# Hybrid attention layer on one core: biases and evictions' stores over ScalarE's queue, later pairs' values in four blocks, decay ranks stored split

## The chip, the core and the metric

The kernel runs on one core of a Trainium2 chip. The core has a matrix engine (TensorE, PE in the profile, with PEld for its weight loads), a vector engine (VectorE, DVE), an activation engine (ScalarE, ACT), a general one (GpSimd, POOL) and one that only issues transfers (SyncE, SP). Each engine works through its own instructions in order and waits on semaphores for the others. DMAs between HBM and the on-chip memory are instructions too: they stand in the queue of the engine that issues them, and the 16 DMA engines of the core do the moving. The metric is the device time of one execution in microseconds.

## The reference, cut to what matters

One encoder layer on 1024 tokens (a grid of 16 rows and 64 columns) of width 1024, in float32: a half-step FFN, a mixer, a half-step FFN, each followed by a scaled residual and a layer norm. The mixer adds two branches, neighbourhood attention (8 heads, a window of 8 x 16 tokens, a bias for each relative offset) and gated linear attention (GLA, 4 heads, two directions), each gated by its own sigmoid:

```python
def reference(x, ...):
    x = layer_norm(ALPHA * x + 0.5 * swiglu_ffn(x, ...), ln1_g, ln1_b)
    x = layer_norm(ALPHA * x + hybrid_mixer(x, w_in, ...), ln2_g, ln2_b)
    x = layer_norm(ALPHA * x + 0.5 * swiglu_ffn(x, ...), ln3_g, ln3_b)

def hybrid_mixer(h, w_in, na_rpb, ...):
    proj = h @ w_in
    na_q, na_k, na_v, g_q, g_k, g_v, g_g, dlf, dlb, gate_na, gate_gla = split(proj)
    y_na = neighborhood_attention(na_q, na_k, na_v, na_rpb) @ w_branch_na
    y_gla = gla_bidirectional(g_q, g_k, g_v, g_g, dlf, dlb, ...) @ w_branch_gla
    merged = sigmoid(gate_na) * y_na + sigmoid(gate_gla) * y_gla
    return merged @ w_out

# neighbourhood attention, per query: scores over its 8 x 16 keys
scores = einsum('bhqd,bhiqjd->bhqij', q_r, k_sel) + bias
p = softmax(scores); out = einsum('bhqij,bhiqjd->bhqd', p, v_sel)
# GLA: decay gates of low rank, per direction
log_a = log_sigmoid(dec_lr @ w_dec2 + b_dec) / 16
```

## The kernel before

Every float32 matmul is done as three: an operand is split into a rounded part and the rest (`split`, L130: ScalarE copies, VectorE subtracts), and high x high, high x low and low x high are added in PSUM. A unit of such work over 512 columns is a "step" of three matmuls; the kernel counts time in such steps (`STEP` = 0.65 units each).

**What sets the order.** TensorE's instructions stand in program order. The code for the dense matmuls are generators that yield after each step; `run` (L189) advances a clock by the step's cost and, when it has passed the time of an entry in a list (`at`, L184), lets that entry write its instructions there. So attention and GLA are threaded between dense matmuls by a table of numbers: `NA_T0` and `NA_DT` for the attention, `GLA_*` for GLA. The instructions of the other engines, DMAs among them, are placed by a scheduler.

**The mixer's stages.** After the first FFN, `tok_major` (L855) computes the attention's values by token and stores them to `vscr`; `decay_rank` (L956) computes the 32 decay ranks and stores them to `dls`; `pairs` (L882) computes queries, keys and the rest. Then comes the attention stage (L1127 to L1134). Its dense work, through which the attention is threaded, is `tok_major` for GLA's values (stored to `gv`, 8 tiles) and four `gate_gla` (stored to `gts`). Each tile of 128 x 512 is evicted by ScalarE into a buffer `sl` (two of them, `stage`, L425) and stored from there by a DMA on SyncE's queue (L877, L1125).

**The attention.** There are 64 items: four pairs of heads, for each two halves of the grid's rows, four blocks of columns, two heads. Item i goes through a chain of engines: `na_scores` (L1047: two matmuls on TensorE, the bias added and the minimum taken on VectorE, the exponential on ScalarE, the normalisation on VectorE), two items later `na_transpose` (L1076: three transposes on TensorE into `pt`, copied out by ScalarE), and an item after that `na_values` (L1087). One item begins every `NA_DT` units. The bias of an item comes from HBM (`bias_tile`, L1039, into `bt`, two buffers), 288 or 384 KB for two or four items; it is asked for when the bias before it comes into use:

```python
if hh == 0 and b != 2:
    na_b[0] = na_b.pop("next")
    if i < 62:
        bias_tile(i + (2 if b != 1 else 4))
```

**The pairs.** `qk_pair` (L1000) loads a pair's queries, keys and values: 13 DMAs for `q`, `k` and `kl` on GpSimd's queue (L1006), and 16 for the values `vp` on SyncE's queue (L1027 to L1031), each of 96 or 128 rows of 512 bytes. For pairs 1 to 3 this happens 10.5 items before the pair's first; GpSimd writes a mark into each tile first (L1010 to L1014), which holds the DMAs back until the item reached by then has its softmax.

**GLA's start.** After the attention, the decay ranks come back from `dls` and are split into a tile `dlT` (L1161 to L1168: two DMAs, four copies on ScalarE, two subtractions on VectorE). `gla_decay` (L1175) of the first head multiplies them (`zs`, L1188) at `GLA_D0`, and at `GLA_T0` the head's first transposes (`kps`, L1224) need the outcome of that chain; the next heads follow every `GLA_DT`.

Of the kernel before, what the change touches and what calls it, by code (L numbers as in the profile page):

```python
# [8 lines left out]
F32 = mybir.dt.float32  # L9
F32R = mybir.dt.float32r  # L10
BF16 = mybir.dt.bfloat16
U32 = mybir.dt.uint32
AF = mybir.ActivationFunctionType
ALU = mybir.AluOpType
# [4 lines left out]
P = 128  # L19
D = 1024  # L20
S = 1024
KD = D // P
HF = 512
# [12 lines left out]
NEG = -1.0e30  # L36
HOIST = 100
WARM = 30
GLA_D0 = 8.5
GLA_T0 = 29.5  # L40
GLA_DT = 30.3
GLA_NEXT = 8.5
GLA_OUT = (15.0, 28.3, 28.3, 35.5)
NA_T0 = 20.0
NA_DT = 0.94
NA_GATES = (4, 5, 6, 7)
GLA_GATES = (1, 2, 3)
FIRST = (1, 2, 4, 8)
# [12 lines left out]
COL0 = (0, 8, 24, 40)  # L61
COLW = (24, 32, 32, 24)
BOFF = (0, 288, 288, 672)
# [4 lines left out]
def hybrid_layer(ctx, tc, xT, wg1, wu1, wds1, wd1, wg2, wu2, wds2, wd2, wcol, wnv, wgv, wdl, wgate,  # L68
                 wbr, wout, lnp, bias, dec2, bdec, ng, ident_d, masks_d, ln3, outN):
    nc = tc.nc  # L70
# [4 lines left out]
    def pool(stack, name, bufs=1, space=None):  # L75
        kw = dict(name=name, bufs=bufs)
        if space is not None:
            kw["space"] = space
        if space is not DRAM:
            kw["reuse_waits"] = "tile"  # L80
        return stack.enter_context(tc.tile_pool(**kw))
# [9 lines left out]
    dram = pool(ctx, "dram", 1, DRAM)  # L91
# [3 lines left out]
    def nm(s):  # L95
        uid[0] += 1
        return f"{s}_{uid[0]}"
# [32 lines left out]
    def split(src, hi, lo):  # L130
        nc.scalar.activation(hi, src, AF.Copy)  # L131
        nc.vector.tensor_tensor(lo, src, hi.bitcast(F32), ALU.subtract)  # L132
# [29 lines left out]
    for c1 in FIRST:  # L162
        w = slice(c0 * P, c1 * P)
# [20 lines left out]
    def at(delay, fn):  # L184
        uid[0] += 1
        pending.append((clock[0] + delay, uid[0], fn))
        pending.sort(key=lambda e: e[:2])
# [634 lines left out]
    one = Ffn(ffn1, x, xr, half(xT), wg1, wu1, wds1, wd1, 0)  # L822
# [19 lines left out]
    ogs = dram.tile([4, P, S], F32, tag="ogs", name="ogs")  # L842
    gts = dram.tile([KD, P, S], F32, tag="gts", name="gts")

    dls = dram.tile([32, S], F32, tag="dls", name="dls")


    def tok_weights(w_d, n):
# [6 lines left out]
    def tok_major(w_d, dst, alloc=None, wq=None):  # L855
        wq = wq or tok_weights(w_d, 4 if alloc is None else 2)
        for i in range(len(wq) // 2, 4):
            raw = wpool.tile([P, D], F32, tag="raw", name=nm("raw"), bufs=2)
            with tc.high_priority(offset=HOIST):
                nc.sync.dma_start(raw, w_d[i])  # L860
                for o in (0, HF):
                    wq.append(alloc())
                    split(raw[:, o:o + HF], *wq[-1])
        for t in range(8):
            h, c = t // 4, (t % 4) * P
            ps = dps()
            for k in range(KD):
                xh, xl = x1[k][h]
                wh, wl = wq[k]
                a, b = xh[:, c:c + P], xl[:, c:c + P]  # L870
                nc.tensor.matmul(ps, a, wh, start=k == 0, stop=False)
                nc.tensor.matmul(ps, a, wl, start=False, stop=False)
                nc.tensor.matmul(ps, b, wh, start=False, stop=k == KD - 1)
                yield STEP
            sb = stage()
            nc.scalar.activation(sb, ps, AF.Copy)
            nc.sync.dma_start(dst(t), sb)  # L877

    unblk = lambda t: t.rearrange("p (b r c) -> p r b c", r=8, b=4)

# [75 lines left out]
    def decay_rank():  # L956
        raw = wpool.tile([P, KD, 32], F32, tag="raw", name=nm("raw"), bufs=2)
        nc.sync.dma_start(raw, wdl)
        w = wpool.tile([P, KD, 64], F32R, tag="wh", name=nm("wh"))
        nc.scalar.activation(w[:, :, 0:32], raw, AF.Copy)  # L960
        nc.vector.tensor_tensor(w[:, :, 32:64], raw, w[:, :, 0:32].bitcast(F32), ALU.subtract)
        for h in range(2):
            ps = dps((64, HF))
            for k in range(KD):
                xh, xl = x1[k][h]
                if k:
                    nc.tensor.matmul(ps[0:32], w[:, k - 1, 0:32], x1[k - 1][h][1], start=False,
                                     stop=False)
                if k == KD - 1:
                    nc.tensor.matmul(ps[0:32], w[:, k, 0:32], xl, start=False, stop=False)  # L970
                nc.tensor.matmul(ps, w[:, k], xh, start=k == 0, stop=k == KD - 1)
                yield STEP * 2 / 3
            sb = stage()
            nc.scalar.activation(sb[0:32], ps[32:64], AF.Copy)
            nc.vector.tensor_tensor(sb[0:32], sb[0:32], ps[0:32], ALU.add)
            nc.sync.dma_start(dls[:, h * HF:(h + 1) * HF], sb[0:32])

    run(tok_major(wnv, lambda t: vscr[t * P:(t + 1) * P, :], one.hpair))
    assert not pending
# [13 lines left out]
    vgrid = vscr.rearrange("(r c) e -> r c e", c=64)  # L993
    nap = ExitStack()
    npool = pool(nap, "npool")
    o_na = [[None, None] for _ in range(4)]
    grid = lambda t: t.rearrange("p (r c) -> p r c", c=64)
    pair = {}

    def qk_pair(p, mark=None):  # L1000
        k2 = [npool.tile([P, S], F32R, tag="k2", name=nm("k2"), bufs=4) for _ in range(2)]
        kl = npool.tile([P, S], F32R, tag="kl", name=nm("kl"), bufs=2)
        vp = npool.tile([P, 16, P], F32, tag="vp", name=nm("vp"), bufs=2)
        q2 = [[None, None], [None, None]]
        pair[p] = (q2, k2, kl, vp)
        load = lambda dst, src: nc.gpsimd.dma_start(dst.bitcast(F32), src)  # L1006
        for h in range(2):
            for hh in range(2):
                q2[hh][h] = npool.tile([P, HF], F32R, tag="q2", name=nm("q2"), bufs=8)
        if mark is not None:  # L1010
            m = mark[:, 0:1]
            for t in (*k2, kl, *q2[0], *q2[1]):
                nc.gpsimd.tensor_copy(t[:, 0:1], m)
            nc.gpsimd.tensor_copy(vp[:, :, 0:1], m.unsqueeze(2).to_broadcast([P, 16, 1]))  # L1014
        for h in range(2):
            hs = slice(h * HF, (h + 1) * HF)
            for hh in range(2):
                a, o = slice(64 * hh, 64 * hh + 64), slice(64 - 64 * hh, 128 - 64 * hh)
                t = q2[hh][h]
                load(t[a], qks[p, 0, a, hs])  # L1020
                load(t[o], qks[p, 1, a, hs])
                if h == 0:
                    load(k2[hh][a], qks[p, 2, a])
                    load(k2[hh][o], qks[p, 2, a])
            if h == 0:
                load(kl, qks[p, 3])
        for b in range(4):  # L1027
            w = COLW[b]
            for g in range(4):
                nc.sync.dma_start(vp[:4 * w, 4 * b + g, :],  # L1030
                                  vgrid[4 * g:4 * g + 4, COL0[b]:COL0[b] + w, p * P:(p + 1) * P])  # L1031


    na_e, na_t, na_b, na_o, na_mark = {}, {}, {}, {}, {}
# [4 lines left out]
    def bias_tile(i):  # L1039
        p, rb, _, b = na_idx(i)  # L1040
        nk = 12 * COLW[b]
        bt = npool.tile([P, 2, 384], F32, tag="bt", name=nm("bt"), bufs=2)
        nc.sync.dma_start(bt[:, :, :nk], bias[p, rb, :, 2 * BOFF[b]:2 * BOFF[b] + 2 * nk]
                          .rearrange("q (h k) -> q h k", h=2))
        na_b["next"] = bt

# [71 lines left out]
    def gate_gla(j):  # L1118
        w = load_w(wgate[KD + j], D)
        for h in range(2):  # L1120
            ps = dps()
            yield from mm_steps(ps, w, x1h[h])
            sb = stage()
            nc.scalar.activation(sb, ps, AF.Copy)
            nc.sync.dma_start(gts[j, :, h * HF:(h + 1) * HF], sb)  # L1125

    bias_tile(0)  # L1127
    qk_pair(0)
    for p in range(1, 4):
        at(NA_T0 + (16 * p - 10.5) * NA_DT, lambda p=p: qk_pair(p, na_mark[0]))  # L1130
    na_events(0, 67, NA_T0, NA_T0 + 67 * NA_DT)
    run(tok_major(wgv, lambda t: gv[t], wq=wq), *[gate_gla(j) for j in NA_GATES])
    flush()
# [2 lines left out]

    gla = ExitStack()
    gp = pool(gla, "gp")
    dec2r = gp.tile([96, 4, P], F32, tag="sq", name="dec2r")
    nc.sync.dma_start(dec2r, dec2)  # L1140
    dec2t = gp.tile([96, 4, P], F32R, tag="dec2", name="dec2t")
# [16 lines left out]
    az = [gp.tile([P, HF], F32, tag=f"az{i}", name=f"az{i}") for i in range(2)]  # L1158
    for t in az:
        nc.gpsimd.memset(t, 0.0)  # L1160
    dlT = gp.tile([96, S], F32R, tag="dlT", name="dlT")  # L1161
    for h, tag in enumerate(("on", "gst")):
        hs = slice(h * HF, (h + 1) * HF)
        dlr = gp.tile([32, HF], F32, tag=tag, name=nm("dlr"), bufs=h + 1)
        nc.sync.dma_start(dlr, dls[:, hs])
        nc.scalar.activation(dlT[0:32, hs], dlr, AF.Copy)
        nc.scalar.activation(dlT[64:96, hs], dlr, AF.Copy)
        nc.vector.tensor_tensor(dlT[32:64, hs], dlr, dlT[0:32, hs].bitcast(F32), ALU.subtract)  # L1168
    ch = lambda t: t.rearrange("p (n c) -> p n c", c=P)
    heads = [dict() for _ in range(4)]  # L1170

# [155 lines left out]

    at(GLA_D0, lambda: gla_decay(0))
    for hd in range(4):
        b = GLA_T0 + GLA_DT * hd  # L1330
        add = lambda t, f, *a: at(b + t, lambda: f(*a))
# [6 lines left out]
        if hd < 3:  # L1338
            add(GLA_NEXT, gla_decay, hd + 1)
        for i, t in enumerate(GLA_OUT):  # L1340
            add(t, (gla_out, gla_otrans)[i % 2], hd, i // 2)
# [164 lines left out]
```

## Time and profile before

| what | value |
|---|---|
| three runs | 2175.60, 2175.74 (median), 2176.88 us |
| the profiled execution | 2175.62 us, its span 2173.7 us |
| VectorE busy | 1377.6 us (63%) |
| ScalarE busy | 901.7 us (41%) |
| GpSimd busy | 161.3 us (7%) |
| HBM traffic | 144 GB/s over the span |

TensorE is busy nearly throughout, so the places where it isn't are what to look for. They lie together in the attention stage. In stretches of 20 us, TensorE's busy time there is:

| stretch (us) | PE busy | granted clock | DMA busy share |
|---|---|---|---|
| 880 to 900 | 19.83 | 1.00 | 0.80 |
| 900 to 920 | 8.51 | 0.66 | 0.36 |
| 920 to 940 | 19.95 | 1.00 | 0.66 |
| 940 to 960 | 5.78 | 0.55 | 0.32 |
| 960 to 980 | 19.90 | 0.94 | 0.30 |
| 980 to 1000 | 18.03 | 1.00 | 0.77 |
| 1000 to 1020 | 6.06 | 0.50 | 0.42 |
| 1020 to 1040 | 20.00 | 0.99 | 0.32 |
| 1040 to 1060 | 16.88 | 1.00 | 0.68 |
| 1060 to 1080 | 8.05 | 0.57 | 0.36 |
| 1080 to 1120 | 40.00 of 40 | 1.00 | 0.24 |

Four holes stand out, each after a stretch in which the DMA engines were busy with a pair's loads. How to read the rows shown further down: a row of waits names the waiting instruction, what it waited for, the sum in us, how often, and the longest; a row of the timeline gives start, duration, engine, line, operation, tiles (out <- in), how many were merged, and in brackets the idle time before it with what ended it.

### The profile page before, as it was taken

To read this page: it belongs to the slowest core of one execution; us is meant where nothing else is said; L and a number is where in the kernel's file an instruction comes from. 1 tells how busy PE (TensorE), PEld (TensorE's weight loads), DVE (VectorE), ACT (ScalarE), POOL (GpSimd) and SP (SyncE) were. 2 spreads that over 40 slices of the span, in tenths; PEclk is the share of its full clock that TensorE was granted. 3 is DMA by queue.
4 is the path that set the end of the run, shared out by engine and by line. 5 is a ranking of instruction groups with operands and counts; after the bars stand their busy time and mean duration, and the time that the engine had idled before them with its cause. 6 is when DMAs were issued, how large, how long until landed. Compare 5 with 4: busy or idle time off the path is not lost. (4 is left out here: it accounts for less than half of the span.)

```text
span 2173.7 us, 26722 instructions
## 1 busy us (share of the span) xinstructions
PE 2084.4 (96%) x9722; PEld 1695.7 (78%) x9722; DVE 1377.6 (63%) x2356; ACT 901.7 (41%) x1506; POOL 161.3 (7%) x228
## 2 busy tenths in 40 slices
PE   9999999999999999777799999999999999999997
PEld 7888888888887788554467888887788888888887
DVE  8667776466678763133346774788877677547647
ACT  6444454312235543233356562535544444322212
POOL 0000000000024121111100000014100000000001
PEclk9999999999999999888899999999999999999999
DMA  4434443596521342545432333622144344386632
GB/s 149 149 136 160 155 159 114 186 343 212 169 61 39 138 161 105 138 118 144 125 110 78 117 122 119 222 90 87 68 147 174 135 162 138 118 289 237 235 112 78
DMA packets 156164, 315.07 MB, mean 145 GB/s; under 512 B 17312, under 2 KB 41632, under 8 KB 156032
## 3 DMA queue, kind: packets, MB, share of 16 engines
q1 hardware_dynamic: 146880, 283.99, 38.6%
q0 software_dynamic: 9152, 29.37, 4.7%
q8 instruction: 77, 1.26, 0.2%
q14 instruction: 55, 0.45, 0.1%
HBM read 216.16 MB, written 97.12 MB: 144 GB/s over the span
## 5 line engine op out<-in xcount | busy, mean ns | idle before, releaser
L131 ACT ACTIVATE wh<-raw 128x512 fp32r<-128x512 f32 (+4 forms) x148 | 111.6, 763 | 195.0 <-PE d L560 85.3
L132 DVE TENSOR_TENSOR wl<-raw,wh 128x512 fp32r<-128x512 f32 (+4 forms) x148 | 125.2, 854 | 103.2 <-ACT wh L131 103.1
L122 PE MATMUL d<-xh,wh 128*128 128x512 f32 x384 | 159.9, 416 | 0.5 <-ACT xh L131 0.3
L681 DVE TENSOR_TENSOR a<-a,d 128x512 f32<-128x512 f32 (+1 forms) x152 | 99.9, 657 | 90.8 <-PE d L561 60.1
L123 PE MATMUL d<-xl,wh 128*128 128x512 f32 x384 | 151.7, 395 | 1.0 <-POOL xl L412 0.5
L124 PE MATMUL d<-xh,wl 128*128 128x512 f32 x384 | 152.0, 396 | 0.5 <-DVE wl L112 0.5
L559 PE MATMUL d<-a,wh 128*128 128x512 f32 x384 | 149.8, 390 | 2.4 <-DVE hr L587 1.6
L561 PE MATMUL d<-xh,wl 128*128 128x512 f32 x384 | 149.5, 389 | 0.5 <-DVE wl L132 0.5
L560 PE MATMUL d<-a,wh 128*128 128x512 f32 x384 | 149.4, 389 | 0.0
L559 PE MATMUL d<-xh,wh 128*128 128x512 f32 x384 | 149.4, 389 | 0.0
L560 PE MATMUL d<-xl,wh 128*128 128x512 f32 x384 | 149.4, 389 | 0.0
L561 PE MATMUL d<-a,wl 128*128 128x512 f32 x384 | 149.4, 389 | 0.0
L559 PE MATMUL d<-hh,hh 128*128 128x512 f32 x384 | 149.4, 389 | 0.0
L560 PE MATMUL d<-hl,hh 128*128 128x512 f32 x384 | 149.4, 389 | 0.0
L561 PE MATMUL d<-hh,hl 128*128 128x512 f32 x384 | 149.4, 389 | 0.0
L131 ACT ACTIVATE hh<-sr 128x512 fp32r<-128x512 f32 x168 | 105.9, 631 | 87.7 <-DVE sr L500 26.0
L659 PE MATMUL d<-hh,wh 128*128 128x512 f32 (+1 forms) x368 | 134.3, 365 | 0.0
L661 PE MATMUL d<-hh,wl 128*128 128x512 f32 (+1 forms) x368 | 133.0, 361 | 0.0
L660 PE MATMUL d<-hl,wh 128*128 128x512 f32 (+1 forms) x368 | 133.0, 361 | 0.0
L132 DVE TENSOR_TENSOR hl<-sr,hh 128x512 fp32r<-128x512 f32 x168 | 114.2, 694 | 1.5 <-ACT hh L131 0.6
L112 DVE TENSOR_TENSOR wl<-raw,wh 128x512 fp32r<-128x512 f32 (+1 forms) x77 | 77.9, 1012 | 55.1 <-ACT wh L111 39.8
L111 ACT ACTIVATE wh<-raw 128x512 fp32r<-128x512 f32 (+1 forms) x77 | 67.5, 878 | 104.0 <-PE d L123 42.0
(336 smaller groups left out, 4923.2 us busy)
## 6 DMA issues: line engine op xcount, KB each, us to landing
raw<-in_wu SPq DMA_DIRECT2D x44, 512.0 KB
raw<-in_wg SPq DMA_DIRECT2D x43, 512.0 KB
ops<-oh SPq DMA_DIRECT2D x84, 256.0 KB
ops<-ol SPq DMA_DIRECT2D x84, 256.0 KB
oh<-ops SPq DMA_DIRECT2D x48, 256.0 KB
ol<-ops SPq DMA_DIRECT2D x48, 256.0 KB
hid<-oh SPq DMA_DIRECT2D x40, 256.0 KB
hid<-ol SPq DMA_DIRECT2D x40, 256.0 KB
```

What stands on the lines that cost most here:

```text
L122: nc.tensor.matmul(ps, a, xh, start=k == 0, stop=False)
L123: nc.tensor.matmul(ps, a, xl, start=False, stop=False)
L124: nc.tensor.matmul(ps, wl[:, k * m:(k + 1) * m], xh, start=False, stop=k == n - 1)
L131: nc.scalar.activation(hi, src, AF.Copy)
L132: nc.vector.tensor_tensor(lo, src, hi.bitcast(F32), ALU.subtract)
L559: nc.tensor.matmul(ps, a, xh, start=first and k == 0, stop=False, **sg)
L560: nc.tensor.matmul(ps, a, xl, start=False, stop=False, **sg)
L561: nc.tensor.matmul(ps, wl[:, k * P:(k + 1) * P], xh, start=False, stop=k == n - 1, **sg)
L659: nc.tensor.matmul(ps, wh, hi, start=k == 0, stop=False)
L660: nc.tensor.matmul(ps, wh, lo, start=False, stop=False)
L661: nc.tensor.matmul(ps, wl, hi, start=False, stop=k == n - 1)
L681: nc.vector.tensor_tensor(a, a, ps, ALU.add)
```

## The change

Five edits:

1. The attention's biases are loaded over ScalarE's queue instead of SyncE's, into three buffers instead of two.
2. The stores behind ScalarE's evictions in `tok_major` (to `vscr` and `gv`) and `gate_gla` (to `gts`) are issued by ScalarE too.
3. The values of pairs 1 to 3 no longer come with queries and keys: a new function `v_block` loads one block of columns with four DMAs, behind a mark of its own, at 9.5, 7.5, 5.5 and 3.5 items before the pair's first. Pair 0 has all four blocks at its start.
4. `decay_rank` splits the ranks itself and stores three parts of 32 rows; GLA's start loads them with one DMA straight into `dlT`.
5. The table: the attention begins 2 units earlier with 0.97 instead of 0.94 units for an item; GLA's decay 2.5 units and its first transposes 2 units earlier, its heads 31.0 instead of 30.3 units apart.

```diff
-GLA_D0 = 8.5
-GLA_T0 = 29.5
-GLA_DT = 30.3
+GLA_D0 = 6.0
+GLA_T0 = 27.5
+GLA_DT = 31.0
 GLA_NEXT = 8.5
-GLA_OUT = (15.0, 28.3, 28.3, 35.5)
-NA_T0 = 20.0
-NA_DT = 0.94
+GLA_OUT = (15.0, 28.8, 28.8, 35.5)
+NA_T0 = 18.0
+NA_DT = 0.97
...
-    dls = dram.tile([32, S], F32, tag="dls", name="dls")
+    dls = dram.tile([96, S], F32, tag="dls", name="dls")
...
             nc.scalar.activation(sb, ps, AF.Copy)
-            nc.sync.dma_start(dst(t), sb)
+            nc.scalar.dma_start(dst(t), sb)
...
-            nc.sync.dma_start(dls[:, h * HF:(h + 1) * HF], sb[0:32])
+            hi, lo = one.tmp(), one.tmp()
+            split(sb[0:32], hi[0:32].bitcast(F32R), lo[0:32].bitcast(F32R))
+            for i, t in enumerate((hi, lo, hi)):
+                nc.sync.dma_start(dls[32 * i:32 * i + 32, h * HF:(h + 1) * HF], t[0:32])
...
-            nc.gpsimd.tensor_copy(vp[:, :, 0:1], m.unsqueeze(2).to_broadcast([P, 16, 1]))
...
-        for b in range(4):
-            w = COLW[b]
-            for g in range(4):
-                nc.sync.dma_start(vp[:4 * w, 4 * b + g, :],
-                                  vgrid[4 * g:4 * g + 4, COL0[b]:COL0[b] + w, p * P:(p + 1) * P])
+
+    def v_block(p, b, mark=None):
+        vp, w = pair[p][3], COLW[b]
+        if mark is not None:
+            nc.gpsimd.tensor_copy(vp[:, 4 * b:4 * b + 4, 0:1],
+                                  mark[:, 0:1].unsqueeze(2).to_broadcast([P, 4, 1]))
+        for g in range(4):
+            nc.sync.dma_start(vp[:4 * w, 4 * b + g, :],
+                              vgrid[4 * g:4 * g + 4, COL0[b]:COL0[b] + w, p * P:(p + 1) * P])
...
-        bt = npool.tile([P, 2, 384], F32, tag="bt", name=nm("bt"), bufs=2)
-        nc.sync.dma_start(bt[:, :, :nk], bias[p, rb, :, 2 * BOFF[b]:2 * BOFF[b] + 2 * nk]
+        bt = npool.tile([P, 2, 384], F32, tag="bt", name=nm("bt"), bufs=3)
+        nc.scalar.dma_start(bt[:, :, :nk], bias[p, rb, :, 2 * BOFF[b]:2 * BOFF[b] + 2 * nk]
...
-            nc.sync.dma_start(gts[j, :, h * HF:(h + 1) * HF], sb)
+            nc.scalar.dma_start(gts[j, :, h * HF:(h + 1) * HF], sb)
...
+    for b in range(4):
+        v_block(0, b)
     for p in range(1, 4):
-        at(NA_T0 + (16 * p - 10.5) * NA_DT, lambda p=p: qk_pair(p, na_mark[0]))
+        t0 = NA_T0 + (16 * p - 10.5) * NA_DT
+        at(t0, lambda p=p: qk_pair(p, na_mark[0]))
+        for b in range(4):
+            at(t0 + (1 + 2 * b) * NA_DT, lambda p=p, b=b: v_block(p, b, na_mark[0]))
...
+    dlT = gp.tile([96, S], F32R, tag="dlT", name="dlT")
+    nc.sync.dma_start(dlT.bitcast(F32), dls)
...
-    dlT = gp.tile([96, S], F32R, tag="dlT", name="dlT")
-    for h, tag in enumerate(("on", "gst")):
-        hs = slice(h * HF, (h + 1) * HF)
-        dlr = gp.tile([32, HF], F32, tag=tag, name=nm("dlr"), bufs=h + 1)
-        nc.sync.dma_start(dlr, dls[:, hs])
-        nc.scalar.activation(dlT[0:32, hs], dlr, AF.Copy)
-        nc.scalar.activation(dlT[64:96, hs], dlr, AF.Copy)
-        nc.vector.tensor_tensor(dlT[32:64, hs], dlr, dlT[0:32, hs].bitcast(F32), ALU.subtract)
```

Three places of the instruction order. The first is ScalarE's at the start of the attention: the first three evictions of GLA's values (`sl<-d`) and the first exponentials (`e`). Before:

```order
L906 ACTIVATE hr_7347<-d_7215 128x512
L876 ACTIVATE sl_7418<-d_7393 128x512
L876 ACTIVATE sl_7446<-d_7421 128x512
L876 ACTIVATE sl_7474<-d_7449 128x512
L1069 ACT_TABLE_LOAD
L1069 ACTIVATE e_7504,sm_7505<-e_7504,sm_7505 128x288
L876 ACTIVATE sl_7513<-d_7477 128x512
L1069 ACTIVATE e_7523,sm_7524<-e_7523,sm_7524 128x288
```

The same place in the changed kernel (`bt<-in_bias` are the biases, `gv<-sl` the stores; line numbers below the new function are some 6 higher):

```order
L1049 DMA bt_7502<-in_bias 128x768
L876 ACTIVATE sl_7430<-d_7405 128x512
L1049 DMA bt_7537<-in_bias 128x2x288
L877 DMA gv<-sl_7430 128x512
L876 ACTIVATE sl_7458<-d_7433 128x512
L877 DMA gv<-sl_7458 128x512
L876 ACTIVATE sl_7486<-d_7461 128x512
L877 DMA gv<-sl_7486 128x512
L1075 ACT_TABLE_LOAD
L1075 ACTIVATE e_7507,sm_7508<-e_7507,sm_7508 128x288
L1075 ACTIVATE e_7522,sm_7523<-e_7522,sm_7523 128x288
L1049 DMA bt_7662<-in_bias 128x2x288
```

Each store now stands right behind its eviction. Two more biases (after a first one just ahead of these rows) are asked for before the attention begins, and `bt_7662`, the fourth bias, which items 8 and 9 use, stands right behind the exponential of item 1.

The second place is SyncE's queue from the attention's first loads to pair 1. Before (an `x4` or `x8` are so many DMAs in a row; `vp_7619` are pair 1's values):

```order
L1030 DMA vp_7359<-vscr 96x1x128 x4
L877 DMA gv<-sl_7418 128x512
L877 DMA gv<-sl_7446 128x512
L1043 DMA bt_7499<-in_bias 128x768
L877 DMA gv<-sl_7474 128x512
L1043 DMA bt_7538<-in_bias 128x2x288
L877 DMA gv<-sl_7513 128x512
L1043 DMA bt_7676<-in_bias 128x2x288
L1030 DMA vp_7619<-vscr 96x1x128 x4
L1030 DMA vp_7619<-vscr 128x1x128 x8
L1030 DMA vp_7619<-vscr 96x1x128 x4
L877 DMA gv<-sl_7687 128x512
```

In the changed kernel (`vp_7622` are pair 1's values):

```order
L1036 DMA vp_7371<-vscr 96x1x128 x4
L1036 DMA vp_7371<-vscr 128x1x128 x8
L1036 DMA vp_7371<-vscr 96x1x128 x4
L1036 DMA vp_7622<-vscr 96x1x128 x4
L1036 DMA vp_7622<-vscr 128x1x128 x8
L1036 DMA vp_7622<-vscr 96x1x128 x4
L110 DMA raw_8761<-in_wgate 128x1024
L110 DMA raw_9039<-in_wgate 128x1024
```

Stores and biases are gone from between and behind the values; what is behind them now are weights for later matmuls.

The third place is TensorE's order around the attention's first score (`s`, of keys `k` and `kl`), inside the fourth tile of GLA's values. Before:

```order
L871 MATMUL d_7477<-wh_7210,xh_5552 128x512
L872 MATMUL d_7477<-wl_7211,xh_5552 128x512
L873 MATMUL d_7477<-wh_7210,xl_5553 128x512
L1061 MATMUL s_7501<-k_1480_7356,q_1484_7360 128x288
L1063 MATMUL s_7501<-kl_7358,q_1484_7360 128x288
L871 MATMUL d_7477<-wh_7210,xh_5569 128x512
```

In the changed kernel:

```order
L871 MATMUL d_7489<-wh_7210,xh_5499 128x512
L872 MATMUL d_7489<-wl_7211,xh_5499 128x512
L873 MATMUL d_7489<-wh_7210,xl_5500 128x512
L1067 MATMUL s_7504<-k_1484_7368,q_1488_7372 128x288
L1069 MATMUL s_7504<-kl_7370,q_1488_7372 128x288
L871 MATMUL d_7489<-wh_7216,xh_5512 128x512
```

The score came after seven of the tile's eight steps and now comes after four, that is nine matmuls earlier.

## The prediction

> **What bounds the kernel now.** I begin with the page's shares and slices.
>
> ```profile
> span 2173.7 us, 26722 instructions
> ...
> PE 2084.4 (96%) x9722; PEld 1695.7 (78%) x9722; DVE 1377.6 (63%) x2356; ACT 901.7 (41%) x1506; POOL 161.3 (7%) x228
> ...
> PE   9999999999999999777799999999999999999997
> ...
> PEclk9999999999999999888899999999999999999999
> ```
>
> TensorE is the bound, except in slices 17 to 20 (870 to 1087 us), where both its busy share and its granted clock fall. That is the attention stage. Next, the waits of TensorE, VectorE and ScalarE from 840 to 1150 us:
>
> ```profile
> PE pt L1081 <- DVE sm L1071: 45.2, 3, 15.9
> PE pt L1081 <- DVE e L1072: 11.7, 1, 11.7
> ...
> DVE e L1067 <- DMA bt<-in_bias: 50.4, 3, 17.6
> ...
> ACT sl L876 <- DMA gv<-sl: 21.4, 1, 21.4
> ```
>
> TensorE loses 45.2 + 11.7 = 56.9 us in four waits, each time because the transposes of an item find no softmax yet. Three times VectorE had waited for a bias. The single one has ScalarE behind it, which waited 21.4 us for a store to free a buffer `sl`, with the first exponentials queued behind. The timeline says why both transfers were late:
>
> ```profile
> 878.51 25.24 SPq L1030 DMA_DIRECT2D vp<-vscr  x16
> 903.86 0.88 SPq L877 DMA_DIRECT2D gv<-sl  x2
> ...
> 924.83 22.15 SPq L1030 DMA_DIRECT2D vp<-vscr  x16
> 947.10 0.39 SPq L877 DMA_DIRECT2D gv<-sl  x1
> 947.60 0.96 SPq L1043 DMA_DIRECT2D bt<-in_bias  x2
> ...
> 952.12 0.56 DVE L1067 CUSTOM_DVE_ANT_0 e<-s,bt 128x384 f32<-128x384 f32 x1 [15.98 <-DMA bt<-in_bias]
> ...
> 954.22 0.87 PE L1081 MATMUL pt<-ident,e 128*128 128x128 f32 x3 [14.27 <-DVE sm L1071]
> ```
>
> Sixteen value loads hold SyncE's queue for 22 to 25 us. The first store goes out at 903.86, and in pair 1 the bias at 947.60, each only when the last value load has been issued. VectorE starts 4.5 us after the bias was issued, TensorE 6.6 us after. The limit of this stage is one issuing queue.
>
> **The waits that go.** Biases and stores leave SyncE's queue. In the changed order the fourth bias stands behind the exponential of item 1 and is used by item 8, and this lead of five to seven items repeats: the third buffer allows it, and what frees a buffer is a VectorE instruction that ScalarE has waited for already. An item lasts:
>
> ```profile
> 1037.57 0.56 DVE L1067 CUSTOM_DVE_ANT_0 e<-s,bt 128x384 f32<-128x384 f32 x1 [0.77 <-PE s L1063]
> ...
> 1039.11 0.42 DVE L1072 TENSOR_SCALAR e<-e,sm 128x384 f32<-128x384 f32 x1
> ...
> 1050.15 0.46 DVE L1067 CUSTOM_DVE_ANT_0 e<-s,bt 128x288 f32<-128x288 f32 x1 [0.75 <-PE s L1063]
> ```
>
> Five items pass from 1037.57 to 1050.15, 2.5 us each, so the lead is some 12 us or more against the 4.5 us that a bias took at 947.60. A store goes out right behind its eviction, and its buffer is due again two tiles later. I take all four waits away: **-56.9 us**.
>
> **The slow clock behind them.** The first four rows are the stretches behind the four waits, the others a pair's load burst, its tail, and pair 0's loads. The columns are the stretch, its length, the busy time of PE, PEld, DVE, ACT and POOL with counts, the granted clock, the DMA engines' busy share, and GB/s:
>
> ```profile
> 911.50:924.00 12.50, 12.50 (x52) 8.37 (x54) 4.55 (x16) 4.70 (x13) 0.26 (x3) 0.74 0.07 27
> 954.20:964.00 9.80, 9.78 (x37) 6.59 (x38) 2.66 (x11) 2.80 (x7) 0.00 (x0) 0.58 0.11 30
> 1013.90:1024.00 10.10, 10.06 (x43) 7.03 (x43) 3.13 (x12) 3.34 (x9) 0.00 (x0) 0.68 0.11 33
> 1072.00:1082.00 10.00, 10.00 (x43) 6.94 (x43) 3.77 (x12) 4.24 (x11) 0.00 (x0) 0.68 0.26 82
> 924.70:937.70 13.00, 13.00 (x78) 9.12 (x77) 4.90 (x18) 6.16 (x16) 6.88 (x14) 1.00 0.96 224
> 940.00:947.00 7.00, 0.00 (x0) 0.00 (x0) 0.00 (x0) 0.00 (x0) 0.00 (x0) 0.63 0.29 79
> 878.00:896.00 18.00, 18.00 (x81) 14.92 (x80) 0.00 (x0) 1.20 (x2) 6.56 (x13) 1.00 0.92 210
> ```
>
> In the first four TensorE is busy without a gap, at a lower clock. A full clock would save length times missing share: 12.5 x 0.26 + 9.8 x 0.42 + 10.1 x 0.32 + 10 x 0.32 = 3.25 + 4.12 + 3.23 + 3.20. Without the waits the clock does not fall: **-13.8 us**. The Trainium skill ("TensorE: Matmul & The Clock Gate", Part 1) says that about 3.4 us of sustained work lift the throttle; by that, four restarts at half speed would cost an estimated 4 x 1.7 = 6.8 us, and the forecast would be 7 us higher. The rows here show more than that page, so they decide.
>
> **A wait that comes.** Pair 0's `kl`: its issue, how long it took to land, and the first matmul that reads it:
>
> ```profile
> 883.54 0.58 POOL L1006 DMA_DIRECT2D kl<-qks  x1 [1.34 <-DMA q<-qks]
> ...
> DMA to landing us min/median/max: 12.5/12.5/12.5
> ...
> 896.50 0.39 PE L1063 MATMUL s<-kl,q 64*128 64x288 f32 x1
> ```
>
> It landed at 896.04, half a microsecond before its use. The first score now comes nine matmuls earlier; 81 of them filled the 18 us before 896, 0.22 us each, so it is due at about 894.5. That alone is a wait of 1.5 us. Besides, ScalarE's queue adds transfers to that burst: two more biases (384 and 288 KB by their shapes) and two stores (256 KB), 1.2 MB. At the stretch's 210 GB/s, with the engines 0.92 busy, that is up to 5.6 us more. I take 4 of them, as `kl` lies ahead of the burst's last loads, so a wait of 5.5, and behind it a loss to the clock near the mildest above, 3.5: **+9.0 us**. The ends are 1.5, and 1.5 + 5.6 + 4.1 = 11.2.
>
> For pairs 1 to 3 the same sharing does no harm: the loads begin 10.5 items, 26 us, ahead. In the changed order GpSimd writes the marks of the value blocks behind its 13 loads, so these blocks are issued as the burst ends; sixteen at the median of 0.72 us (next fence) are through 12 us later, and TensorE reads them four items into the pair at the earliest.
>
> **ScalarE's own time.** This trace has no DMA on ScalarE. The nearest rows are SyncE's, a bias and a value load, and the value loads that met pair 1's burst:
>
> ```profile
> L1043 SPq DMA_DIRECT2D bt<-in_bias x24: 327/379/454, 878.1 to 1108.5; - x24
> ...
> L1030 SPq DMA_DIRECT2D vp<-vscr x64: 526/720/9143, 878.5 to 1063.6; - x64
> ...
> L1030 SPq DMA_DIRECT2D vp<-vscr x5: 526/2846/6173, 927.5 to 938.0; - x5
> ...
> L1030 SPq DMA_DIRECT2D vp<-vscr x2: 2846/2944/3042, 934.9 to 938.0; - x2
> ```
>
> A DMA holds its engine between 0.33 and 9.14 us. I take 0.38, since it is the same transfer. The attention adds 24 biases and 16 stores, 15 us of ScalarE. They lie beside TensorE: two items are 5.0 us, and from the bias's addition to the end of the normalisation (1037.57 to 1039.53) an item needs 2.0, so ScalarE may be up to 3 us late. Cost nothing; the other end is a rival below. The eight `vscr` stores and the split of the decay ranks, a few ScalarE and VectorE instructions under dense matmuls, cost nothing either; without cover, 8 x 0.38 = 3 us.
>
> **GLA's start.** TensorE's waits from 1130 to 1310 us, the longest and the two that the change touches:
>
> ```profile
> PE kps L1224 <- ACT ket L1226: 2.8, 2, 1.4
> PE zs L1188 <- DVE dlT L1168: 1.0, 1, 1.0
> PE zs L1188 <- ACT dlT L1167: 0.9, 1, 0.9
> ```
>
> With `dlT` loaded whole, 1.0 + 0.9 go: **-2.0 us**. The transposes behind that chain keep 21.5 units after it instead of 21, so nothing new should wait. Ends: -4.7 (all three gone) and +2 (the gain turned into a wait at `kps`).
>
> **The sum**, from the profiled execution (2175.62 us: the span and 1.9 around it; 0.1 under the median): 2175.6 - 56.9 - 13.8 + 9.0 - 2.0 = 2111.9, so **2112 us**. With the ends: 2175.6 - 70.7 + 1.5 - 4.7 = 2102, and 2175.6 - 70.7 + 11.2 + 2 + 3 = 2121.
>
> **Rivals.**
>
> *ScalarE is held.* While a burst fills the DMA engines (0.96 busy from 924.7 to 937.7), three value loads of pair 1 held SyncE for 6.2, 3.0 and 2.8 us. If ScalarE's next DMA is held as long, exponentials behind it are late. One hold in each pair costs 3 x (6.2 - 3) = 10 us, giving 2122; all three in a row cost 3 x (12.0 - 3 + 3.5) = 38, giving 2150. For it: biases and stores do fall into bursts. Against: the value loads now come as the burst ends. The Trainium skill ("Perfetto Trace Analysis", DMA Instruction — HWDGE) says that the sequencers issuing such DMAs share one descriptor generator and lock it; this trace, with one such engine, cannot show it.
>
> *The change doesn't do what it says: the biases stay late.* Were the DMA engines the limit, a queue of its own would help only until the burst is over. The bias would then land 4.5 us after 937.7, 9.9 us earlier than at 952.1, and of pair 1's 14.3 us wait 4.4 would stay, with 3.5 for the clock: 3 x 7.9 = 24 us, giving 2136. Against: from 940 to 947, when the bias still waited, the engines were 0.29 busy, and the lead is long. The skill ("DMA: Bandwidth & Descriptors", Issuing engines are not separate DMA queues) leans this way: another issuer saves issue time alone. Here issue time was the wait.
>
> *Slower than before.* One mechanism: every DMA on ScalarE in the attention stage holds it, in a burst or not. 40 holds eat the gain of 63.7 us when each costs 1.6 beyond the 3 us of slack, so from 4.6 us each. At 6.2 it would be 40 x 3.2 = 128 us: 2240. For it there is only the longest row; the median of 0.72 speaks against.
>
> **How the numbers follow.** My forecast has 0.62, ScalarE held 0.19, biases late 0.10, slower 0.06, and 0.03 is left for gains and losses that cancel. The range must leave out no more than 0.2: it takes the forecast's 2102 to 2121, the late biases, and the lower part of the held ScalarE, to 2138; with 1 us below for the profile's rounding, 2101 to 2138. A measurement of this kernel can tell about 0.2% (4 us) from no change. Faster: 0.62 + 0.19 + 0.10 = 0.91; slower 0.06; the same 0.03.
>
> **What would show it.** Right: no wait of `pt` for the softmax above 1 us, none of VectorE for `bt`, a granted clock of 1.00 from 910 us to the stage's end; one wait of the first score for `kl` of about 5 us; DMAs on ScalarE of about 0.4 us; no wait of `zs` for `dlT`. Wrong: rows of several us for ScalarE's DMAs (first or third rival), VectorE still waiting for `bt` (second), values that TensorE waits for, or `kl` landing as early as before (2104).

## The result, and the profile after

| kernel | median (us) | lowest and highest | runs |
|---|---|---|---|
| before | 2175.67 | 2173.28 to 2176.88 | 4 |
| changed | 2114.12 | 2112.51 to 2115.14 | 4 |

The ratio is 0.9718, with a 95% interval of 0.9701 to 0.9735: the kernel is 61 us faster. The forecast was 2112. The profiled execution of the changed kernel took 2112.51 us. In the experiments further down, one run with the biases alone (7336.55 us) and one of the kernel before (2363.05 us, beside GLA's start) stand far above the others, and the ratios leave them out.

First the page of the changed kernel, shares and slices:

```profile
span 2110.7 us, 26717 instructions
...
PE 2073.1 (98%) x9722; PEld 1688.4 (80%) x9722; DVE 1379.8 (65%) x2356; ACT 898.4 (43%) x1503; POOL 163.0 (8%) x237
...
PE   9999999999999999989999999999999999999997
...
PEclk9999999999999999999999999999999999999999
```

Of four weak slices one is left, slice 18 (897 to 950 us). Its waits of TensorE, between 840 and 1330 us (waiting instruction, what it waited for, sum, times, longest):

```profile
PE pt L1087 <- DVE e L1078: 5.5, 1, 5.5
PE s L1069 <- DMA kl<-qks: 3.5, 1, 3.5
...
PE kps L1229 <- DVE gz L1216: 0.6, 1, 0.6
PE zs L1193 <- DVE st L1243: 0.6, 1, 0.6
```

The waits for `sm`, 45.2 us before, are gone. The one of 11.7 us before, at the first softmax, is still there with 5.5, and the first score has the wait for `kl` that was forecast. The last two rows are all that is left at GLA's start. The stretches of the changed kernel, with the same columns as in the prediction, show the clock (last but two):

```profile
880.00:900.00 20.00, 16.45 (x70) 13.19 (x69) 0.47 (x2) 1.20 (x2) 4.58 (x9) 0.96 0.89 215
900.00:920.00 20.00, 14.46 (x67) 9.48 (x67) 5.51 (x20) 8.40 (x19) 0.59 (x5) 0.78 0.27 88
920.00:1080.00 160.00, 159.98 (x970) 112.10 (x967) 75.63 (x251) 86.05 (x209) 31.50 (x81) 1.00 0.59 166
898.00:904.00 6.00, 4.59 (x12) 2.81 (x11) 0.93 (x4) 0.03 (x1) 0.00 (x0) 0.72 0.29 89
908.10:918.00 9.90, 9.86 (x46) 6.96 (x46) 3.72 (x14) 4.18 (x10) 0.00 (x0) 0.79 0.20 68
```

From 920 to 1080 us, where three pairs are loaded, TensorE is busy for 159.98 of 160 us at full clock. What is lost lies in pair 0. The timeline there, of ScalarE and of TensorE's waits:

```profile
879.62 1.06 ACTq L1049 DMA_DIRECT2D bt<-in_bias  x2
880.73 0.60 ACT L876 ACTIVATE sl<-d 128x512 f32<-128x512 f32 x1 [4.32 <-PE d L873]
893.77 0.39 ACTq L1049 DMA_DIRECT2D bt<-in_bias  x1
894.25 0.42 ACTq L877 DMA_DIRECT2D gv<-sl  x1
894.72 0.60 ACT L876 ACTIVATE sl<-d 128x512 f32<-128x512 f32 x1 [13.39 <-DMA q<-qks]
...
897.76 0.40 PE L1069 MATMUL s<-kl,q 64*128 64x288 f32 x1 [3.55 <-DMA kl<-qks]
...
903.54 0.33 ACTq L877 DMA_DIRECT2D gv<-sl  x1
903.98 0.60 ACT L876 ACTIVATE sl<-d 128x512 f32<-128x512 f32 x1 [8.66 <-DMA vp<-vscr]
...
906.85 0.54 ACT L1075 ACTIVATE e<-e,sm 128x288 f32<-128x288 f32 x1
...
908.14 0.88 PE L1087 MATMUL pt<-ident,e 128*96 128x128 f32 x3 [5.54 <-DVE e L1078]
```

ScalarE's DMAs are short rows (0.33 to 0.54 us), but before the bias at 893.77 ScalarE does nothing for 12.4 us, and between 895.3 and 903.5 nothing for 8.2 us. The gap stands in brackets at the next computing instruction. The first score was done at 898.2, and its exponential begins at 906.85, behind a third eviction. So **ScalarE was held in pair 0**, which the forecast had as a rival.

The difference of the two profiled executions, from these rows and those in the prediction:

| part | forecast | measured |
|---|---|---|
| four waits of `pt` | -56.9 | -56.9 + 5.5 = -51.4 |
| clock behind them | -13.8 | -13.8 + 2.1 (9.9 x 0.21) = -11.7 |
| wait for `kl` | +5.5 | +3.5 |
| clock behind it | +3.5 | +1.3 (4.59 busy x 0.28) |
| GLA's start | -2.0 | from 6.0 (the 4.7 shown and 0.8 + 0.5) to 1.2 us of waits: -4.8 |
| sum | -63.7 | -63.1 |

The spans differ by 63.0 us.

### The profile page after: what moved, and what is told of

The parts are those of the page before. It is cut to its first block, busy times and chain, and to the rows that moved or that the text cites. A ratio compares the mean times of both kernels' runs of the same rounds, so it can differ in the third digit from the quotient of the medians.

```text
span 2110.7 us, 26717 instructions
## 1 busy us (share of the span) xinstructions
PE 2073.1 (98%) x9722; PEld 1688.4 (80%) x9722; DVE 1379.8 (65%) x2356; ACT 898.4 (43%) x1503; POOL 163.0 (8%) x237
## 4 chain that ended last, share of the span: by engine, by line
PE 80%; issue 7%; DVE 7%; DMA 3%; ACT 2%; POOL 2%; SPq 0%; ACTq 0%; DVEq 0%; POOLq 0%
PE d L559 16%; PE d L561 16%; PE d L560 16%; PE d L122 5%; PE d L123 5%; PE d L124 5%; PE d L659 3%; PE d L661 3%; PE d L660 3%; PE pt L1087 1%; PE po L1105 1%; PE s L1069 1%; DMA sb<-gts 1%; DMA bt<-in_bias 1%; PE d L871 1%
## 5 line engine op out<-in xcount | busy, mean ns | idle before, releaser
L131 ACT ACTIVATE oh<-hr 128x512 fp32r<-128x512 f32 x88 | 55.4, 631 | 131.0 <-DVE hr L588 49.0
```

## The experiments

All kernels ran beside the kernel before; ratios are to it. An interval of a ratio is 2.4 to 4.1 us to either side, so differences below about 5 us between two kernels are read from traces, not from times.

### Which edit brings the time

Three kernels have one edit alone, two are the changed kernel with one edit undone, and one has a smaller part undone.

**Biases alone** (kernel before, edit 1):

```diff
-        bt = npool.tile([P, 2, 384], F32, tag="bt", name=nm("bt"), bufs=2)
-        nc.sync.dma_start(bt[:, :, :nk], bias[p, rb, :, 2 * BOFF[b]:2 * BOFF[b] + 2 * nk]
+        bt = npool.tile([P, 2, 384], F32, tag="bt", name=nm("bt"), bufs=3)
+        nc.scalar.dma_start(bt[:, :, :nk], bias[p, rb, :, 2 * BOFF[b]:2 * BOFF[b] + 2 * nk]
```

> The kernel before with edit 1 alone: biases over ScalarE's queue into three buffers, everything else as before. Theory A (each late transfer was late only because it stood behind sixteen value loads in SyncE's queue): the three waits for a bias go with their clock loss, 45.2 + 10.6 us, and the first one, for a store, stays: 2175.7 - 55.8 = 2120 us. Theory B (the moved DMAs are held too, on ScalarE, while a burst is under way): the exponentials are late in each pair and 10 us or more of the three waits remain: 2130 us or more.

Measured: 2162.66 us, 0.9941 (0.9924 to 0.9957). Theory A, which was the forecast's, falls. VectorE waits for no bias any more, but TensorE now waits for ScalarE's copies:

```profile
PE pt L1081 <- ACT et L1084: 28.2, 6, 7.8
PE pt L1081 <- DVE e L1072: 8.4, 1, 8.4
```

**Stores alone** (kernel before, edit 2; the same at L1125 for `gts`):

```diff
-            nc.sync.dma_start(dst(t), sb)
+            nc.scalar.dma_start(dst(t), sb)
```

> The kernel before with edit 2 alone: the evictions' stores over ScalarE's queue. Theory A: the first wait goes with its clock loss, 11.7 + 3.3 us, the three for a bias stay: 2161 us. Theory B: ScalarE's first stores wait for earlier transfers of pair 0 to land, as they do in the changed kernel, and some 5 us of wait before the first transposes plus 3 us of clock stay: 2169 us.

Measured: 2169.11 us, 0.9975 (0.9964 to 0.9986), as Theory B had it: the wait for the first softmax fell from 11.7 only to 7.5 us. The three waits for `sm` stayed (48.2 us), as both theories said.

**The changed kernel with the values in one go** (edit 3 undone: one mark before queries and keys, all blocks at once):

```diff
+            nc.gpsimd.tensor_copy(vp[:, :, 0:1], m.unsqueeze(2).to_broadcast([P, 16, 1]))
...
-            at(t0 + (1 + 2 * b) * NA_DT, lambda p=p, b=b: v_block(p, b, na_mark[0]))
+            at(t0, lambda p=p, b=b: v_block(p, b))
```

> The changed kernel without edit 3: the sixteen value loads of a pair come with its queries and keys again, on SyncE's queue. Theory A: nothing urgent is behind them in that queue any more, so the time stays: 2114 us, within 4. Theory B: with the burst fuller, DMAs on ScalarE wait for earlier ones in each of pairs 1 to 3, several us each: 2125 us or more.

Measured: 2163.72 us, 0.9949 (0.9932 to 0.9965). The edit to which the forecast gave nothing is worth 50 us here.

**Values in blocks alone** (kernel before, edit 3):

> The kernel before with the third edit alone: the values of pairs 1 to 3 in four blocks behind marks of their own; biases and stores stay on SyncE's queue. Theory A (the blocks alone free the queue, since undoing them cost 50 us): the four waits of the transposes go, 2115 to 2125 us. Theory C (all three edits are needed together: SyncE takes its instructions in order, so biases behind the sixteen value loads are now also behind the marks that these wait for): the waits of VectorE for `bt` stay, some longer, and the time is 2160 to 2185 us.

Measured: 2143.94 us, 0.9872 (0.9855 to 0.9889). Both theories missed. The waits of VectorE for `bt` fell from 50.4 to 6.8 us, so the blocks alone do much; TensorE still waited 11.1 us for the first softmax (before 11.7) and 13.4 us in four waits in the pairs, and the stretches of 20 us with these four have a granted clock of 0.74 to 0.91. The sixteen loads of pair 1 hold SyncE for 10.7 us in place of 22.2, and the biases go out behind them:

```profile
936.35 10.66 SPq L1033 DMA_DIRECT2D vp<-vscr  x16
947.11 0.97 SPq L1046 DMA_DIRECT2D bt<-in_bias  x2
```

**The changed kernel with the stores back on SyncE** (edit 2 undone):

> The changed kernel with the second edit undone: all stores of the evictions are on SyncE's queue again, behind the value loads and their marks. Theory A (the stores on ScalarE are needed): an eviction waits for its buffer in the pairs, ScalarE is late with exponentials, and the time is 2122 to 2140 us. Theory C' (the stores are what holds ScalarE in pair 0, and the biases alone had to move): the hold of 8.7 us behind the second store goes, and the time is 2106 to 2113 us.

Measured: 2122.41 us, 0.9773 (0.9758 to 0.9787), the lower end of Theory A's time, but not where it had it. The price lies for the most part in pair 0: the wait of `pt` for the first softmax is 10.4 instead of 5.5 us, with ScalarE waiting 14.9 us for a store to free its buffer.

**Two bias buffers instead of three** in the changed kernel:

> The changed kernel with two bias buffers instead of three: the third early bias no longer stands ahead of the first store in ScalarE's queue, and later biases are asked for one bias later. Theory A (12.4 us of ScalarE's wait in pair 0 belong to that third bias): the wait before the first transposes shrinks, the later biases still arrive: 2108 to 2114 us. Theory B (the wait is for earlier transfers to land, whoever asks): it moves to the first store, 2114 us; if biases become late in each pair, 2120 us or more.

Measured: 2118.32 us, 0.9741 (0.9726 to 0.9755). The median is 4.2 us higher and the intervals overlap, so the third buffer is worth little; the hold in pair 0 stays (ScalarE waits 12.6 and 8.8 us), as Theory B had it.

Together, as gains over the median of before (one minus the ratio, times 2175.7):

| edits present | gain (us) |
|---|---|
| 1 | 12.8 |
| 2 | 5.4 |
| 3 | 27.8 |
| 1, 2, 4, 5 | 11.1 |
| 1, 3, 4, 5 | 49.4 |
| all | 61.4 |

Edit 3 alone and the rest without it give 38.9 together; some 22.5 come only when both are there (each gain is uncertain by some 3.5).

### Why the queue alone was not enough

The kernel with the biases alone, in the timeline around pair 1's loads: two biases on ScalarE, SyncE's value loads between, the instruction behind the second bias, and TensorE's wait on it.

```profile
924.25 0.35 ACTq L1043 DMA_DIRECT2D bt<-in_bias  x1
...
925.15 17.51 SPq L1030 DMA_DIRECT2D vp<-vscr  x9
...
936.06 0.37 ACTq L1043 DMA_DIRECT2D bt<-in_bias  x1
936.54 0.49 ACT L1084 ACTIVATE et<-pt 96x384 f32<-96x384 f32 x1 [7.74 <-DMA vp<-vscr]
...
937.08 0.87 PE L1081 MATMUL pt<-ident,e 128*96 128x128 f32 x3 [5.23 <-ACT et L1084]
```

ScalarE stood still for 7.7 us until a *value load* of SyncE had landed, although the bias has nothing to do with values. The program's own list of waits says why. SyncE's queue, then ScalarE's (numbers are places in each engine's order; DMAHW0 to 7 are completion counters):

```
413 L1030 DMA vp_7619<-vscr 96x1x128 [waits DMAHW2_49,Pool_49]
414 L1030 DMA vp_7619<-vscr 96x1x128 [waits DMAHW3_49]
415 L1030 DMA vp_7619<-vscr 96x1x128 [waits DMAHW5_49]
416 L1030 DMA vp_7619<-vscr 96x1x128 [waits DMAHW6_49]
```

```
621 L1043 DMA bt_7727<-in_bias 128x768 [waits DMAHW4_49]
626 L1043 DMA bt_7778<-in_bias 128x2x288 [waits DMAHW5_49,DMAHW2_49]
```

There are eight counters for the DMAs of both engines, dealt out in turn: SyncE's list leaves out the 4 that ScalarE's bias 621 has taken. Each DMA waits until the former one on its counter has landed. The bias in row 626 is the one at 936.06; its own counter is 5, and the DMA before it there is value load 415, the third of the burst. The trace has that load issued at 926.51, among queries and keys, and its counter full at 935.99, 0.07 us before the bias goes out. (Counter 2 stands for the former bias in the same buffer, which had landed before the burst.) A queue of its own doesn't free a DMA from SyncE's transfers, and on ScalarE the wait also stops the exponentials.

The same, larger, in the changed kernel with the values in one go (waits of ScalarE, then of TensorE):

```profile
ACT et L1091 <- DMA vp<-vscr: 31.2, 4, 12.5
ACT e L1076 <- DMA vp<-vscr: 11.6, 1, 11.6
...
PE po L1106 <- ACT et L1091: 26.2, 3, 11.2
```

In the changed kernel there is no such wait in pairs 1 to 3. For pair 0, where it was held, the list and the trace name two different transfers. The bias at 893.77 has the counter of the first bias, issued by ScalarE itself at 879.62 and landed at 893.69 (the row's `q<-qks` is not what it waits for). The store at 903.54 has the counter of a value load that landed at 903.46.

The Trainium skill ("DMA: Bandwidth & Descriptors", Issuing engines are not separate DMA queues) says that DMAs of several engines run on the same 16 DMA engines and that another issuer saves issue time only. The runs agree in direction: biases alone, stores alone, and both without edit 3 gave 12.8, 5.4 and 11.1 us of 61.4.

**All sixteen loads in one go, but behind queries and keys.** This separates the two things that edit 3 does, the place and the grouping:

```diff
-            at(t0 + (1 + 2 * b) * NA_DT, lambda p=p, b=b: v_block(p, b, na_mark[0]))
+            at(t0 + NA_DT, lambda p=p, b=b: v_block(p, b, na_mark[0]))
```

> The changed kernel with all sixteen value loads of a pair behind their marks at one place, one item behind queries and keys, so that they come in one go but behind GpSimd's thirteen loads. Theory C1 (what made the value loads slow, and ScalarE's DMAs behind them late, was that they were in flight together with queries and keys): time stays at 2112 to 2120 us, and the sixteen are issued in some 12 us. Theory C2 (groups of four, with time between them, are what is needed): ScalarE is held for value loads in pairs 1 to 3 and the time is 2130 to 2165 us.

Measured: 2116.81 us, 0.9741 (0.9723 to 0.976). It is the place: Theory C1's time. The sixteen loads of pair 1 did not go out in 12 us, though; they still took 18.95 us (from 931.15). Their rows are 0.63 us at most; the rest is waiting, where the counters now work the other way: the load at 938.26 went out when a store of ScalarE on its counter had landed (938.25). Yet ScalarE was held in the pairs only this long:

```profile
ACT et L1090 <- DMA vp<-vscr: 3.7, 1, 3.7
```

**Values of pairs 1 to 3 over GpSimd's queue**, whose DMAs have other counters (DMASW), in the kernel with the values in one go:

```diff
+        eng = nc.gpsimd if p else nc.sync
...
-            nc.sync.dma_start(vp[:4 * w, 4 * b + g, :],
+            eng.dma_start(vp[:4 * w, 4 * b + g, :],
```

> The kernel with the values in one go (2163.7 us) with the values of pairs 1 to 3 issued by GpSimd instead of SyncE, at the same place. GpSimd's DMAs have landing counters of their own, the biases and stores of ScalarE share theirs with SyncE's. Theory C (ScalarE is held because its DMA must wait for a value load that has the same counter): the waits of ScalarE for value loads in pairs 1 to 3 go, TensorE's waits behind them as well, and the time is 2112 to 2125 us. Theory D (it is the load on the DMA engines or on their rings, whoever issues): ScalarE's DMAs stay late by as much and the time stays at 2155 to 2168 us.

Measured: 2148.56 us, 0.9892 (0.9875 to 0.9908), outside both. ScalarE's waits for value loads in pairs 1 to 3 are gone, as Theory C has it; but the values now come late, which costs TensorE eight waits:

```profile
PE po L1107 <- DMA vp<-vscr: 16.3, 8, 2.9
```

This run doesn't settle counters against place, since on GpSimd's queue the values also stand behind queries and keys.

### Pair 0, and a faster version

**Pair 0's values staged too**: block 0 at the start, the others behind marks.

```diff
-    for b in range(4):
-        v_block(0, b)
+    v_block(0, 0)
+    for b in range(1, 4):
+        at(NA_T0 + (2 * b - 1.5) * NA_DT, lambda b=b: v_block(0, b, na_mark[0]))
```

> The changed kernel with pair 0's values in blocks too: block 0 at the start, blocks 1 to 3 behind marks from 0.5 to 4.5 items after the attention's first, two items apart. Theory C (pair 0's sixteen value loads at once hold ScalarE by their counters for 12.4 and 8.7 us, and fill the burst that makes `kl` late): the wait of 5.5 us for the first softmax, the wait for `kl` and the slow clock behind them go for the most part, 2101 to 2108 us. Theory D (the burst of queries, keys and biases alone is enough): both waits stay, 2112 to 2116 us; later blocks that come too late would show as waits of `po` for `vp`.

Measured: 2110.51 us, 0.9714 (0.97 to 0.9729), between the two. The waits say which part holds:

```profile
PE s L1069 <- DMA kl<-qks: 3.9, 1, 3.9
PE pt L1087 <- DVE e L1078: 1.5, 1, 1.5
```

Without the twelve value loads ahead of it the third bias is dealt another counter and goes out at 881.04 instead of 893.77, and the wait for the softmax falls from 5.5 to 1.5 us (C). The wait for `kl` stays (D): it comes from queries, keys and biases.

**The attention later and closer**, `NA_T0` 25.5 and `NA_DT` 0.856 in the changed kernel:

> The changed kernel with the attention 7.5 units (about 20 us) later and its items 0.856 units apart instead of 0.97, so that it ends at the same time; pair 0's loads are asked for where they were. Theory C (pair 0's waits come from loads and held instructions that have too little time ahead of the first item): the wait of 3.5 us for `kl`, that of 5.5 us for the first softmax and the 3.4 us of slow clock go, 2100 to 2107 us. Theory D (closer items leave ScalarE and VectorE too little slack in pairs 1 to 3, or the loads of a pair too little time): waits of `pt` and `po` come in the pairs, 2112 to 2130 us.

Measured: 2117.35 us, 0.9742 (0.9723 to 0.9761), in the range of Theory D but hardly for its reason. The wait for `kl` is gone, but the one for the first softmax has grown to 9.4 us; only 0.6 us of this row and one wait of 1.8 us lie in the pairs:

```profile
PE pt L1087 <- DVE e L1078: 9.9, 2, 9.4
```

Two more evictions now stand on ScalarE ahead of the first exponential and wait 3.5 and 1.8 us for stores to free their buffers; it starts at 912.95 instead of 906.85.

**Both together:**

> The two candidates together: pair 0's values staged in blocks (2110.5 us) and the attention 7.5 units later with items 0.856 apart. If the two act on the same waits, it is no faster than the better of them (2100 to 2108 us); if pair 0's later blocks now fall into pair 1's loads (which come closer behind), values come late and it is slower than 2110 us.

Measured: 2108.73 us, 0.971 (0.9691 to 0.9728), the lowest median of all, with 2.4 us of waits of `pt` for the softmax, 1.7 of `po` for a copy, and none for `kl`. It beats the kernel before; against the changed one its span is 4.6 us shorter (2106.1), but the intervals overlap, so that step isn't established.

### GLA's start

**The changed kernel with edit 4 and GLA's part of the table undone:**

> The changed kernel with GLA's start as before: the decay ranks stored once and split after loading, and GLA's part of the table (decay, transposes, distance of the heads, outputs) as it was; the attention's part of the table stays changed. Theory A (the forecast's term: two waits of `zs` for `dlT`, 2.0 us): 2116 us, with 1.0 + 0.9 us of waits back. Theory B (what the two traces show: waits from 1130 to 1310 us fell from 6.0 to 1.2 us): 2119 us, with the waits of `kps` for `ket` back too (2.8 us). Theory D (the waits are hidden elsewhere later): 2114 us.

Measured: 2114.02 us, 0.973 (0.9717 to 0.9744). The median is that of the changed kernel, the ratio 0.0012 higher, 2.6 us and within the intervals: unclear. In its trace `kps` waits again, while `zs` has no wait for `dlT` even so:

```profile
PE kps L1232 <- ACT ket L1234: 2.9, 2, 1.5
```

## Why the prediction was right, and where it was not

- **What bounds the kernel**: right about the place, the four waits and the slow clock behind them. "The limit of this stage is one issuing queue" was too little. SyncE was held inside the rows of its value loads, up to 9.14 us each amid queries and keys; its queue was where this showed. In the changed kernel the longest such row is 2.03 us:

```profile
L1036 SPq DMA_DIRECT2D vp<-vscr x64: 509/611/2034, 877.6 to 1028.0; - x64
```

- **The waits that go**, -56.9: the size was nearly right (-51.4), the reason was not. They were put down to biases and stores leaving SyncE's queue. Alone those edits give 12.8 and 5.4 us, and with both but without edit 3 11.1. The step that failed is "Cost nothing" for the DMAs on ScalarE. The lead of "some 12 us or more" held, for with the biases alone VectorE's 50.4 us of waits for them are gone. But a bias on ScalarE waits for a value load's counter and holds the instructions behind it: TensorE then waited 28.2 us for ScalarE's copies, and 33.8 us (26.2 + 7.6) in the changed kernel with the values in one go. The observation that the value blocks come "as the burst ends" stood in the text, but as an argument against a rival, with no term in the sum; it carried the result.
- **The slow clock**, -13.8: right from 920 to 1080 us; 2.1 came back behind pair 0's remaining wait.
- **The wait that comes**, +9.0: `kl` landed in 13.7 us instead of 12.5, and its wait with its clock was 3.5 + 1.3 = 4.8. The mechanism was right, within the ends given; the value taken was too large. What was missed is the wait beside it: 5.5 us for the first softmax, and 2.1 for the clock.
- **ScalarE's own time**, 0.38 us for each DMA: as rows, right (medians of 0.33 to 0.39). The test given for a held ScalarE, "rows of several us for ScalarE's DMAs", was wrong: here the hold is the idle time ahead of the row.
- **ScalarE is held** (0.19): true in pair 0 of the changed kernel, and in pairs 1 to 3 of the two kernels that have biases on ScalarE and values in one go on SyncE. The reason given against it was the right one.
- **GLA's start**, -2.0: 4.8 us of waits went, and the attribution is open. The waits for `dlT` stay away without edit 4; that for `kps` returns without it and its table.

The total came out within about 2 us because two errors cancelled, which is luck: 3.4 us more in pair 0 (12.4 instead of 9.0) and 2.8 less at GLA's start. The greater luck is that the edit without a term in the sum was part of the change. The same sum without it would still give some 2112 us, where that kernel took 2163.72.

## What to carry to other kernels

Before a DMA is moved to another engine's queue, list what it waits for besides its data: a completion counter shared with slow transfers goes with it, and on an engine that computes the wait stops the computing. Ask first why the queue is slow; here sixteen small loads put behind a burst instead of into it gave more than a second queue, and the two together 22 us more than their sum. A sum that comes out right doesn't show that its terms are: only kernels with one edit each could tell whose gain it was.

## What was not expected of the hardware

- DMAs of SyncE and ScalarE share eight completion counters in this program, and a store on ScalarE waited 12.5 us for a value load of SyncE that it has no data in common with (values in one go). In the changed kernel the row of such a DMA itself stays at 0.33 to 0.54 us.
- Sixteen value loads of 48 or 64 KB took some 22 to 28 us to issue amid a pair's queries and keys, with single rows of up to 10.3 us, and some 11 to 20 us behind them, marks and waits for ScalarE's transfers included. Why they are issued and land so slowly there wasn't measured by itself.
